# A decoder trunk on one core: where eight fixed weight tiles are used, and where a ring of six

## The chip, the core and the metric

The kernel runs on one core of one Trainium2 chip. The metric is device time in microseconds (us) of one execution; a kernel's time is the median of several runs. Profiles are of one execution each. The engines go by the profile's names: PE (matrix products), PEld (its weight loads), DVE and ACT (elementwise work), POOL, and SP, which here issues nearly all transfers from device memory.

## The reference, cut to what matters

Two pre-norm layers over a residual stream of 256 positions by 2048 columns, in 32-bit floats:

```
for layer in range(2):
    xn  = rms_norm(h, norm_mix[layer])
    mix = swa_mlstm_mixer(xn, ...) if layer == 0 else forgetting_attention_mixer(xn, ...)
    h   = h + mix                  # each mixer ends in: concat(heads) @ w_out   (2048 x 2048)
    h   = h + (silu(xn2 @ w_gate) * (xn2 @ w_up)) @ w_down     # xn2 = rms_norm(h, norm_ffn)
return rms_norm(h, norm_final)
```

Layer 0's mixer projects `xn` once and feeds a sliding-window attention (columns 0 to 1023 of the concatenation) and an mLSTM of four heads (columns 1024 to 2047). Layer 1's mixer is a causal attention of 16 heads with a forget-gate bias. An FFN has 5632 hidden columns.

## The kernel before

**A product.** Every operand is split into a rounded part `hi` and a remainder `lo`, and a product of 32-bit floats is three matmuls: `hi` with `hi`, `hi` with `lo`, `lo` with `hi` (L220 to L222 in `gemm`, L530 to L532 in `three`). Weights come in *chunks* of 256 rows by 512 columns (512 KB). SP loads a chunk into a `raw` tile (L132), ACT casts it to `hi` (L185), DVE subtracts to get `lo` (L186). A chunk then serves 12 matmuls of 512 columns: two groups of 128 rows, two halves of the 256 positions, three products. `raw` tiles for plain chunks come from the pool `wr`, four of them, and one is free again when `lo` has been computed.

**Weight slots.** A cast chunk lives in a *slot*, a pair of tiles `hi`, `lo` of 4 KB a partition each. Before the change there are six fixed pairs, made once (L104), and `slot()` (L106) hands them out in turn: a chunk's cast must wait until the matmuls on the chunk that used that pair before are done. `close_layer` (L762) opens a pool `fp`, makes two more fixed pairs in it, `more`, appends them to the six, and so has eight for everything until it ends: the output projection (`out_proj`, L508) and the FFN. Then the two are taken out again.

**Where `more` lies.** Pools are stacked. `fp` begins at the address at which the mixer's pool began (`ev` in layer 0, `od` in layer 1), as that pool has been closed by then. Within a pool, tiles lie in the order in which their tags were first asked for. `more` comes right after `sx` (two tiles of 6 KB) and `x4` (1 KB), so it takes the bytes from 13312 to 29696 of the region. In `od` those bytes hold `vtail`, the forget-gate columns, `qt`, `kt` and most of `tt`, all of them read by the last group of four heads; in `ev` they hold part of `og`, the gates, `alibi` and `dt_`, which the mLSTM reads to its end. The framework makes the first write of a tile wait for the last reader of what lay there.

**Mixers.** `project` streams a column block of 512 through `gemm`, eight chunks. `pair_group` (L537) handles two column blocks at once with eight steps, three or four of them *mixed* (a scheme that trades one of eight products for additions on DVE), the others plain. Each step of a mixer takes two slots.

**Output projection.** `out_proj` goes through the four column blocks of `w_out` two at a time. For the first two, called acc 0 and acc 1 here: the first six chunks of acc 0 (rows 0 to 1535), the first six of acc 1, then the last two of acc 0 and the last two of acc 1. In layer 1 the first six chunks of a block need none of the last group of heads; in layer 0 the first four need no mLSTM head. A block's matmuls add up in one accumulator, so that its first chunk must come first. Acc 1's first two chunks are the seventh and the eighth to ask for a slot, and with eight pairs they get `more`.

**Order.** The framework orders the instructions of each engine once, when the program is built, by a simulated timeline: an engine takes the earliest instruction in program order among those that are ready. On the chip each engine, SP's queue included, follows that order and waits where it must. The last heads of layer 1 run through scores (L384, L387), exponentials (L418), scaling (L431), transposes (L471, L475), the products with the values (L485, L486) and the split into `mh` and `ml` (L354, L355); layer 0's through L1081 to L1103, transposes on SP (L333) for two heads and on PE (L1130) for the others, and L359, L360.

Of the kernel before, what the change touches and what calls it, by code (L numbers as in the profile page):

```python
# [9 lines left out]
F32R = mybir.dt.float32r  # L10
# [7 lines left out]
P = 128  # L18
# [5 lines left out]
NB = 512  # L24
CK = 2
# [43 lines left out]
def mixed_of(order):  # L69
    return [p for w, p in order if w]  # L70
# [5 lines left out]
def trunk(  # L76
# [23 lines left out]
    xl = sp_.tile([P, KT, S], F32R, name="xl")  # L100
    mh = sp_.tile([P, KT, S], F32R, name="mh")
    ml = sp_.tile([P, KT, S], F32R, name="ml")
    wp = ctx.enter_context(tc.tile_pool(name="wp", bufs=1))
    weights = [[wp.tile([P, CK, NB], F32R, name=f"{a}{i}") for a in ("hi", "lo")] for i in range(6)]  # L104

    def slot():  # L106
        weights.append(weights.pop(0))
        return weights[-1]

    wr = ctx.enter_context(tc.tile_pool(name="wr", bufs=4))  # L110
    cp = ctx.enter_context(tc.tile_pool(name="cp", bufs=1))
# [70 lines left out]
    def split_chunk(raw, n):  # L182
        hi, lo = slot()
        for k in (slice(0, 1), slice(1, CK)) if any(raw is f for f in fine) else (slice(0, CK),):
            latest[0] = nc.scalar.copy(hi[:, k, 0:n], raw[:, k, 0:n])  # L185
            nc.vector.tensor_tensor(  # L186
                out=lo[:, k, 0:n], in0=raw[:, k, 0:n], in1=hi[:, k, 0:n].bitcast(F32), op=ALU.subtract
            )
        return hi, lo
# [318 lines left out]
    def out_proj(w, idx, key, extra):  # L508
        last, rest = KT - 4, []
        for n0 in (0, 2):  # L510
            accs = [new_acc() for _ in range(2)]
            for i in range(2):
                gemm(accs[i], m_of, w, (n0 + i) * NB, NB, 0, last, KT, step=6 * i)
            for i in range(2):
                gemm(accs[i], m_of, w, (n0 + i) * NB, NB, last, KT, KT, step=6)
                add_out(accs[i], n0 + i)
                (later if n0 == 0 else rest).append(
                    (LATER[n0 + i], split_turned(idx, n0 + i, *scrap(extra[3], n0 + i), extra))
                )
                square_sum(key, n0 + i)  # L520
        return rest
# [15 lines left out]
    def pair_group(fp, par, lhs, sums, mats, order, todo=(), halves=None, inner=None, raws=None):  # L537
# [32 lines left out]
        for pos, (kind, pair) in enumerate(order):  # L570
# [21 lines left out]
            if first:  # L592
# [8 lines left out]
                else (t4[:, 0, :], t4[:, 1, :], ra[:, 0, :], ra[:, 1, :])  # L601
            )
            hu, lu = slot()
            split_plain(hu[:, 1, :], lu[:, 1, :], rb[:, 1, :])
            nc.vector.tensor_tensor(out=ta, in0=rb[:, 0, :], in1=ra[:, 0, :], op=ALU.subtract)
# [4 lines left out]
            for src in (ra, rb) if halves else (t4, ra):  # L610
                if halves:
                    hs, ls = halves.pop(0)
                    halves.append((hs, ls))
                else:
                    hs, ls = slot()
                split_plain(hs, ls, src)
                parts.append((hs, ls))
# [144 lines left out]
    def close_layer(layer, w_out, idx, key, **rest):  # L762
        with tc.tile_pool(name=f"fp{layer}", bufs=2) as fp:
            nx = len(mixed_of(ORDER))
            nd = max(len(mixed_of(o)) for o in DOWN.values())
            sx = [fp.tile([P, nx, 4, P], F32R, name=f"sx{i}", bufs=1) for i in range(2)]
            x4 = fp.tile([P, 2, P], F32R, name="x4", bufs=1)
            more = [[fp.tile([P, CK, NB], F32R, name=f"{a}{i}", bufs=1) for a in ("hi", "lo")] for i in (6, 7)]
            weights.extend(more)
            todo = out_proj(w_out, idx, key, (*sx, x4, fp))  # L770
            sd = [fp.tile([P, nd, 4, P], F32R, tag=f"sd{i}", name=f"sd{i}", bufs=1) for i in range(2)]
            ffn(layer, fp, sx, x4, sd, key, todo, **rest)
            for pair in more:
                weights.remove(pair)


    acc0 = new_acc()
    hi, lo = slot()
# [366 lines left out]
    for n in range(4):  # L1145
        nc.gpsimd.dma_start(h[:, :, n * NB : (n + 1) * NB], xv[:, :, n * NB : (n + 1) * NB])

    close_layer(0, w_out_even[0], 2, "f0", idx_next=1, key_next="m1")


# [140 lines left out]
    def finish(acc, n, gf):  # L1291
        for t in range(NT):
# [31 lines left out]
            nc.scalar.dma_start(ov[:, t, NB : 2 * NB], b1)  # L1324

    close_layer(1, w_out_odd[0], 3, "f1", finish=finish)


# [47 lines left out]
```

## Time and profile before

| | |
|---|---|
| median of 3 runs | 2105.7 us (2105.07 to 2107.09) |
| profiled execution, own time | 2104.5 us |
| its span | 2102.8 us |
| PE busy, share of the span | 2072.5 us, 99% |
| DVE, ACT busy | 1821.5 us (87%), 1373.8 us (65%) |
| device memory read | 408.68 MB, 195 GB/s |
| mean granted PE clock | 0.993 |

How to read it: a row of the windows view gives a stretch of time in us from the span's start, then each engine's busy time in it with the number of instructions in brackets, the granted clock of PE as a share of full speed, the DMA engines' busy share and the rate. A row of the timeline gives start, duration, engine, line, operation, out<-in, shape and count, and in square brackets the engine's idle time before it with what ended it. The profiled execution's own time is 1.7 us longer than its span; the rest lies outside what the profile shows. PE counts as busy while any of its pipelined matmuls is under way.

### The profile page before, as it was taken

How to read it: one execution, taken by the hardware profiler on the slowest of the kernel's cores; microseconds unless marked ns; L12 is line 12 of the kernel's file. 1: busy time of each engine (PE TensorE's matmuls, PEld its weight loads, DVE VectorE, ACT ScalarE, POOL GpSimd, SP SyncE). 2: the span in 40 equal slices, each digit the busy share in tenths (PEclk: the TensorE clock that was granted, in tenths of full speed). 3: DMA queues.
4: the chain of work that ended last, by engine and by line, in shares of the span. 5: the costliest groups of instructions: out<-in, count | busy, mean ns of one | idle time of the engine just before them, and what ended most of it. 6: DMA issues, size and time to landing. Idle time of an engine off the chain costs nothing.

```text
span 2102.8 us, 26924 instructions
## 1 busy us (share of the span) xinstructions
PE 2072.5 (99%) x9473; PEld 1718.5 (82%) x9473; DVE 1821.5 (87%) x2367; ACT 1373.8 (65%) x1744; POOL 41.4 (2%) x66
## 2 busy tenths in 40 slices
PE   9999899999999999999999999899999999999998
PEld 7878688888888888888888888688888888888887
DVE  6788668999999899999898778579999999899994
ACT  6767577665576656667676776577655667556763
POOL 1010100000000000000000000000000000000000
PEclk9999999999999999999999999899999999999999
DMA  8566577666677567766677866476756677666763
GB/s 291 178 200 200 170 230 218 214 210 200 207 224 227 185 202 227 229 202 181 213 214 193 242 184 193 135 237 204 240 192 225 196 209 225 216 200 206 224 193 139
DMA packets 309576, 434.87 MB, mean 207 GB/s; under 512 B 106413, under 2 KB 114625, under 8 KB 309313
## 3 DMA queue, kind: packets, MB, share of 16 engines
q1 hardware_dynamic: 307088, 426.27, 66.1%
q0 software_dynamic: 1632, 5.80, 0.8%
q8 instruction: 74, 1.21, 0.2%
q10 hardware_dynamic: 720, 1.09, 0.1%
q14 instruction: 62, 0.50, 0.1%
HBM read 408.68 MB, written 2.12 MB: 195 GB/s over the span
## 4 chain that ended last, share of the span: by engine, by line
PE 94%; ACT 2%; DVE 2%; DMA 1%; issue 1%; SPq 1%; POOLq 0%; POOL 0%; ACTq 0%; DVEq 0%
PE acc L530 20%; PE acc L531 20%; PE acc L532 20%; PE acc L221 5%; PE acc L220 5%; PE acc L222 5%; PE prod L530 5%; PE prod L532 5%; PE prod L531 5%; DVE lo L186 1%; PE p L384 1%; PE po L485 1%; ACT hi L185 1%; ACT s L418 0%; DMA raw<-in_w_out_odd_dram 0%
## 5 line engine op out<-in xcount | busy, mean ns | idle before, releaser
L186 DVE TENSOR_TENSOR lo<-raw,hi 128x1024 fp32r<-128x1024 f32 (+3 forms) x656 | 769.1, 1190 | 159.2 <-ACT hi L185 157.5
L185 ACT CAST hi<-raw 128x1024 fp32r<-128x1024 f32 (+3 forms) x656 | 662.4, 1027 | 353.9 <-PE acc L532 165.3
L531 PE MATMUL acc<-lo,xh 128*128 128x512 f32 x1320 | 513.9, 389 | 0.0
L532 PE MATMUL acc<-hi,xl 128*128 128x512 f32 x1320 | 511.2, 389 | 0.0
L530 PE MATMUL acc<-hi,xh 128*128 128x512 f32 x1320 | 506.2, 390 | 0.0
L532 PEld LDWEIGHTS acc<-hi,xl 128*128 128x128 f32 x1320 | 247.8, 188 | 51.4
L531 PEld LDWEIGHTS acc<-lo,xh 128*128 128x128 f32 x1320 | 247.8, 188 | 51.4 <-issue 0.2
L530 PEld LDWEIGHTS acc<-hi,xh 128*128 128x128 f32 x1320 | 247.8, 188 | 51.4 <-issue 0.2
L354 ACT CAST hi<-raw 128x512 fp32r<-128x512 f32 x204 | 166.9, 819 | 159.5 <-PE acc L532 80.7
L355 DVE TENSOR_TENSOR lo<-raw,hi 128x512 fp32r<-128x512 f32 x204 | 190.2, 932 | 14.0 <-ACT hi L354 12.8
L531 PE MATMUL acc<-lo,mh 128*128 128x512 f32 x466 | 181.3, 389 | 0.0
L532 PE MATMUL acc<-hi,ml 128*128 128x512 f32 x466 | 180.7, 389 | 0.0
L530 PE MATMUL acc<-hi,mh 128*128 128x512 f32 x466 | 176.8, 390 | 1.3 <-ACT hi L185 1.3
L354 ACT CAST hi<-t 128x1024 fp32r<-128x1024 f32 x95 | 100.0, 1053 | 68.6 <-PE acc L532 40.7
L220 PE MATMUL acc<-hi,mh 128*128 128x512 f32 (+1 forms) x322 | 125.4, 393 | 7.8 <-ACT mh L359 7.3
L355 DVE TENSOR_TENSOR lo<-t,hi 128x1024 fp32r<-128x1024 f32 x95 | 115.7, 1218 | 16.1 <-ACT hi L354 15.8
L221 PE MATMUL acc<-lo,mh 128*128 128x512 f32 (+1 forms) x322 | 126.0, 392 | 0.1
L222 PE MATMUL acc<-hi,ml 128*128 128x512 f32 (+1 forms) x322 | 124.5, 392 | 0.0
L530 PEld LDWEIGHTS acc<-hi,mh 128*128 128x128 f32 x466 | 87.3, 188 | 20.2 <-ACT hi L185 2.2
L532 PEld LDWEIGHTS acc<-hi,ml 128*128 128x128 f32 x466 | 87.5, 188 | 18.2
L531 PEld LDWEIGHTS acc<-lo,mh 128*128 128x128 f32 x466 | 87.5, 188 | 18.2
L221 PE MATMUL acc<-lo,xh 128*128 128x512 f32 (+3 forms) x288 | 99.7, 347 | 0.2 <-DVE lo L186 0.2
(356 smaller groups left out, 3171.2 us busy)
## 6 DMA issues: line engine op xcount, KB each, us to landing
raw<-in_w_gate_dram SPq DMA_DIRECT2D x176, 512.0 KB, 4.4
raw<-in_w_up_dram SPq DMA_DIRECT2D x176, 512.0 KB, 4.7
raw<-in_w_down_dram SPq DMA_DIRECT2D x176, 512.0 KB, 4.7
raw<-in_w_in_odd_dram SPq DMA_DIRECT2D x88, 512.0 KB, 5.1
raw<-in_w_in_even_dram SPq DMA_DIRECT2D x51, 512.0 KB, 4.8
raw<-in_w_out_even_dram SPq DMA_DIRECT2D x32, 512.0 KB, 4.5
raw<-in_w_out_odd_dram SPq DMA_DIRECT2D x32, 512.0 KB, 4.4
hr<-in_w_in_even_dram SPq DMA_DIRECT2D x12, 512.0 KB, 4.5
```

Of the source, the lines that this page charges most:

```text
L185: latest[0] = nc.scalar.copy(hi[:, k, 0:n], raw[:, k, 0:n])
L186: nc.vector.tensor_tensor(out=lo[:, k, 0:n], in0=raw[:, k, 0:n], in1=hi[:, k, 0:n].bitcast(F32), op=ALU.subtract)
L220: nc.tensor.matmul(o, ah[:, ts], hi, start=(k == 0), stop=False)
L221: nc.tensor.matmul(o, ah[:, ts], lo, start=False, stop=False)
L222: nc.tensor.matmul(o, al[:, ts], hi, start=False, stop=(k == k_all - 1 and cs.stop == n))
L354: nc.scalar.copy(dst_h, src)
L355: nc.vector.tensor_tensor(out=dst_l, in0=src, in1=dst_h.bitcast(F32), op=ALU.subtract)
L384: nc.tensor.matmul(pq[j % 2][:, j // 2, :], q_of(j, b), k_of(j)[:, 0:cols], start=True, stop=True)
L485: nc.tensor.matmul(po, v_of(j, 0), tt[:, j, 0:2, :].rearrange("p c q -> p (c q)"), start=True, stop=False)
L530: nc.tensor.matmul(o, ah, hi, start=start, stop=False)
L531: nc.tensor.matmul(o, ah, lo, start=False, stop=False)
L532: nc.tensor.matmul(o, al, hi, start=False, stop=stop)
```

## The change

The six fixed pairs go. In their place `wp` is a pool of six buffers per tag, and `slot()` asks it for a new `hi` and a new `lo` whenever `stock` is empty; the pool gives whichever buffer is free, and a new tile's first write waits for the last reader of the tile that had it. `stock` is filled only around `ffn`: with two pairs in `fp`, now made after `out_proj` and after `sd`, and with six pairs taken from the ring. It is emptied when the FFN ends. So mixers and output projections run on the ring of six, and the FFNs on eight fixed pairs as before. `more` no longer lies behind `x4`, but behind everything that `out_proj` has asked of `fp`.

```diff
-    wp = ctx.enter_context(tc.tile_pool(name="wp", bufs=1))
-    weights = [[wp.tile([P, CK, NB], F32R, name=f"{a}{i}") for a in ("hi", "lo")] for i in range(6)]
+    wp = ctx.enter_context(tc.tile_pool(name="wp", bufs=6))
+    stock = []
 
     def slot():
-        weights.append(weights.pop(0))
-        return weights[-1]
+        if not stock:
+            return [wp.tile([P, CK, NB], F32R, tag=a, name=a) for a in ("hi", "lo")]
+        stock.append(stock.pop(0))
+        return stock[-1]
...
             x4 = fp.tile([P, 2, P], F32R, name="x4", bufs=1)
-            more = [[fp.tile([P, CK, NB], F32R, name=f"{a}{i}", bufs=1) for a in ("hi", "lo")] for i in (6, 7)]
-            weights.extend(more)
             todo = out_proj(w_out, idx, key, (*sx, x4, fp))
             sd = [fp.tile([P, nd, 4, P], F32R, tag=f"sd{i}", name=f"sd{i}", bufs=1) for i in range(2)]
+            more = [[fp.tile([P, CK, NB], F32R, name=f"{a}{i}", bufs=1) for a in ("hi", "lo")] for i in range(2)]
+            stock.extend(more + [slot() for _ in range(6)])
             ffn(layer, fp, sx, x4, sd, key, todo, **rest)
-            for pair in more:
-                weights.remove(pair)
+            stock.clear()
```

## The prediction

> **What bounds the kernel now.** I read the page first, then the waits of PE, then windows, then single stretches of the timeline. The page:
>
> ```profile
> span 2102.8 us, 26924 instructions
> PE 2072.5 (99%) x9473; PEld 1718.5 (82%) x9473; DVE 1821.5 (87%) x2367; ACT 1373.8 (65%) x1744; POOL 41.4 (2%) x66
> PE 94%; ACT 2%; DVE 2%; DMA 1%; issue 1%; SPq 1%; POOLq 0%; POOL 0%; ACTq 0%; DVEq 0%
> ```
>
> PE is the bound, and the change neither adds nor removes a matmul, a cast, a subtraction or a byte loaded. So it can only move the time in which PE stands, 2102.8 - 2072.5 = 30.3 us, and the time in which it runs slowly. PE's waits are nearly all in two places:
>
> ```profile
> PE pp L471 <- DVE s L431: 9.5, 1, 9.5
> PE acc L220 <- ACT mh L359: 7.3, 1, 7.3
> ```
>
> Both belong to the step from a mixer to its output projection, in layer 1 and in layer 0. The windows around them (columns: length, PE, PEld, DVE, ACT, POOL busy, clock, DMA share, rate), with the stretches before and after:
>
> ```profile
> 0.00:226.00 226.00, 223.94 (x1173) 184.69 (x1174) 178.23 (x290) 160.83 (x266) 20.41 (x43) 1.00 0.68 216
> 242.00:255.00 13.00, 4.20 (x17) 2.43 (x15) 6.73 (x26) 6.36 (x17) 1.42 (x2) 0.75 0.27 72
> 255.00:260.00 5.00, 5.00 (x17) 3.97 (x18) 3.19 (x9) 3.69 (x11) 0.69 (x1) 0.62 0.48 128
> 260.00:271.00 11.00, 10.82 (x50) 8.28 (x48) 7.83 (x13) 6.02 (x13) 0.69 (x1) 1.00 0.42 134
> 271.00:330.00 59.00, 59.00 (x262) 48.88 (x261) 38.76 (x51) 40.40 (x54) 0.00 (x0) 1.00 0.80 249
> 1050.00:1294.00 244.00, 243.97 (x1149) 204.45 (x1147) 206.72 (x273) 172.78 (x230) 13.71 (x12) 1.00 0.73 206
> 1318.00:1328.00 10.00, 0.47 (x2) 0.18 (x1) 6.18 (x15) 4.66 (x17) 0.00 (x0) 0.62 0.41 136
> 1328.00:1335.00 7.00, 7.00 (x29) 6.04 (x29) 1.99 (x7) 1.76 (x3) 0.00 (x0) 0.57 0.00 0
> ```
>
> The mixers (0 to 226 and 1050 to 1294) leave PE 2.06 and 0.03 us idle: nothing is to be won there. Lost at the two steps is, in layer 0, 13.00 - 4.20 = 8.8 us of standing, 0.2 in the row after next, and 5.00 x (1 - 0.62) = 1.9 us at the low clock; in layer 1, 10.00 - 0.47 = 9.5 us and 7.00 x (1 - 0.57) = 3.0 us. Together 10.9 + 12.5 = **23.4 us**, which is the most that the change can win there.
>
> **Why PE stands there.** I count what the output projection had done. One chunk has four L220 matmuls:
>
> ```profile
> 226.00:242.00 16.00, 6.09 (x16) 3.02 (x16) 1.00 0.73 267
> 242.00:255.00 13.00, 0.15 (x1) 0.15 (x1) 0.75 0.27 72
> 1294.00:1318.00 24.00, 9.55 (x24) 4.51 (x24) 1.00 0.62 190
> 1318.00:1328.00 10.00, 0.00 (x0) 0.00 (x0) 0.62 0.41 136
> ```
>
> These are windows of line 220 alone. In layer 1 it is 24, six chunks: all that acc 0 has without the last heads, and nothing of acc 1, whose six chunks need none of them either. In layer 0 it is 16, four chunks: acc 0's attention heads, and none of acc 1's four. So PE had work with no open operand but the weights. Were they there? The casts of layer 1:
>
> ```profile
> 1315.75 1.04 ACT L185 CAST hi<-raw 128x1024 fp32r<-128x1024 f32 x1 [1.30 <-DVE lo L186]
> 1319.47 1.04 ACT L185 CAST hi<-raw 128x1024 fp32r<-128x1024 f32 x1 [2.67 <-DVE mx L403]
> ...
> 1334.21 0.59 ACT L354 CAST mh<-po 128x512 fp32r<-128x512 f32 x1 [3.01 <-PE po L486]
> 1335.09 0.59 ACT L354 CAST mh<-po 128x512 fp32r<-128x512 f32 x1 [0.29 <-PE po L486]
> 1335.57 2.01 ACT L185 CAST hi<-raw 128x1024 fp32r<-128x1024 f32 x2
> ```
>
> and the last reader of `vtail` and `tt`, beside the two ends of the stall:
>
> ```profile
> 1317.72 0.40 PE L222 MATMUL acc<-hi,ml 128*128 128x512 f32 x1
> 1327.64 1.45 PE L471 MATMUL pp<-ident,s 128*128 128x128 f32 x4 [9.53 <-DVE s L431]
> ...
> 1334.67 0.38 PE L486 MATMUL po<-tt,vtail 128*128 128x128 f32 x2
> ```
>
> SP has loaded ahead:
>
> ```profile
> 1294.42 44.99 SPq L132 DMA_DIRECT2D raw<-in_w_out_odd_dram  x13
> ```
>
> Yet no chunk is cast between 1320.5 and 1335.57; then two are cast back to back, right after the last read of `vtail` and `tt` ends at 1335.05. Acc 1's first two chunks are the seventh and the eighth, and their slots are `more`, on the bytes of `vtail`, `qt`, `kt` and `tt`. I read the two casts as these. Acc 1 cannot begin before its first chunk, so the other four, cast or not, are of no use. Two of the four `raw` tiles are held by them besides, so that the rest of the loading goes through two. In layer 0 the pair comes after the last read of `og`:
>
> ```profile
> 263.27 0.88 DVE L1103 SCALAR_TENSOR_TENSOR hv<-hv,st,og 128x256 f32<-128x256 f32 x2 [0.48 <-POOL st L1101]
> 266.02 1.99 ACT L185 CAST hi<-raw 128x1024 fp32r<-128x1024 f32 x2
> ```
>
> **The change, part by part.**
>
> *The ring in the output projections* takes that wait away: a slot of `wp` depends on matmuls alone. PE gets acc 1's four chunks in layer 0 and six in layer 1. The row 271 to 330 has 59.00 us for 262 matmuls, 0.225 us each, so a chunk costs 12 x 0.225 = 2.7 us: 10.8 us of work in layer 0 for 10.9 us of loss, 16.2 us in layer 1 for 12.5 us. In layer 1 the cover suffices with 3.7 us to spare. In layer 0 it just does, and the mLSTM's instructions have to share ACT and DVE with more casts at that moment (1.0 and 1.2 us each, in the rows of L185 and L186 below), so I take 2 us off. Another 2 us I take off over both for an order of PE that was fixed in advance: a transpose that is queued a little early holds the chunks behind it. Below, the recovery could be nothing (what PE waits for is late by other causes too), above all 23.4. Sum: 23.4 - 2 - 2 = **19.4 us**.
>
> *Eight slots become six there.* Cost nothing, hidden by what is already cast: six chunks are 16.2 us of PE. The longest pause of casts that is not the stall itself is at the end of layer 1's projection, 1396.2 to 1405.83:
>
> ```profile
> 1394.23 2.00 ACT L185 CAST hi<-raw 128x1024 fp32r<-128x1024 f32 x2 [0.26 <-DMA raw<-in_w_up_dram]
> 1405.83 1.04 ACT L185 CAST hi<-raw 128x1024 fp32r<-128x1024 f32 x1
> ```
>
> 9.6 us, within the 16.2. Without that cover the difference, two chunks or 5.4 us a layer, would be the price.
>
> *The ring in the mixers.* The casts there already wait for slots; the groups of lines from 1050 to 1294:
>
> ```profile
> L185 ACT CAST hi<-raw 128x1024 fp32r<-128x1024 f32 (+1 forms) x78 | 76.4, 1004 | 37.0 <-PE acc L532 18.4 <-DMA raw<-in_w_in_odd_dram 15.2 <-issue 1.8
> L186 DVE TENSOR_TENSOR lo<-raw,hi 128x1024 fp32r<-128x1024 f32 (+1 forms) x78 | 89.8, 1169 | 27.7 <-ACT hi L185 27.7
> ```
>
> 18.4 us of ACT's idle time end with a matmul, which costs PE 0.03 us in all. Six pairs stay six pairs; what changes is which buffer a chunk gets, and so possibly the order. No row shows a ring. From below it could win the 2.06 + 0.03 us; from above I see no limit short of the slower case below. I take **+0.5 us**, nearer the windows' zero.
>
> *`more` behind `sd`, eight pairs in the FFNs.* Nothing: when the FFN begins, the mixer's tiles under `more` are long read, and its first two chunks get free pairs. The scraps of the output projection slide forward onto bytes that the last heads read, but they are first written after acc 0 has closed, which needs those heads. SP's queue keeps its entries; loads that waited for the two held `raw` tiles come earlier, and the transposes of L333 and L453 are queued among them as before.
>
> The sum: 19.4 - 0.5 = 18.9 us less. Against the profiled execution's span that is 2102.8 - 18.9 = 2083.9, its own time 2104.5 - 18.9 = 2085.6; the median of the runs is 1.2 us above that execution, so I predict **2087 us**.
>
> **A rule beside it.** The low clock after the stalls is the second term: 0.62 in the 5 us after 7.3 us of standing, 0.57 in the 7 us after 9.5. The Trainium skill, TensorE: Matmul & The Clock Gate, Part 1: The HAM clock gate, says that one idle window of about 3.4 us drops PE to half rate, until it has been busy for about as long. The trace agrees with the drop; by the page's window it would cost 1.7 us each, 3.4 in all, where the rows give 4.9.
>
> **The rivals.**
>
> *The heads stay the bound* (half is won). Acc 1 runs in the gap, but the order of PE puts the transposes (L471) or the first mLSTM chunk where they still wait. For it: the chain from the scores to L431 is long, and SP's transposes in layer 0 take 10.3 us in a row with nothing to shorten them:
>
> ```profile
> 245.84 10.34 SPq L333 DMA_TRANSPOSE hv<-room  x8
> ```
>
> Against it: in the other attentions the same order leaves PE 0.03 us idle over 244 us. Half of 23.4 is 11.7: 2105.7 - 11.7 + 0.5 = 2094.5 us.
>
> *Six slots are too few in the output projections.* Casts wait for PE 18.4 us in 78 there, 0.24 us each; if that fell through to PE in the 64 chunks of both projections, 15 us of the gain would go: 2087 + 15 = 2102 us. Against it: in the mixers, with six, it does not fall through. The Trainium skill, Perfetto Trace Analysis, Optimization Strategy, says that the same gap repeating on the engine that should be full can mean too few buffers; by that rule taking two away is the wrong way. The trace's two gaps do come from a buffer, but from its place.
>
> *The change doesn't do what it says*: acc 1's chunks still come late, since acc 0's fifth and sixth sit in two of six slots until the mLSTM ends. Four slots remain, so it would need the loads to be late as well. 2105.7 us.
>
> *Slower: overtaking in the mixers.* A fixed pair forces chunks into their order; the ring gives a free buffer to whichever cast is ready. In `pair_group` the mixed steps have their own `raw` tiles, loaded far ahead, and can take the buffers of an earlier plain chunk that lands late; PE then stands until a step ends. For it: 15.2 us of ACT's waits there end with a landing, so plain chunks do land late. The place: three mixed steps in each of seven groups, 21. It decides from 18.9 / 21 = 0.9 us each on; at half a chunk, 1.35 us, it is 28 us: 2087 + 28 = 2115 us.
>
> **How the numbers follow.** Chances: forecast 0.64, heads stay the bound 0.20, six too few 0.03, no effect 0.03, overtaking 0.10. A measurement of this kernel can tell about 0.2%, 4.2 us, from no change. Faster: 0.64 + 0.20 = 0.84; within: 0.03 + 0.03 = 0.06; slower: 0.10. The range goes from 2080 (all 23.4 us, the mixers' 2.1) to 2103, which takes in the half case and six too few and leaves out the last two and a little at the bottom. The forecast alone lies within 2080 to 2092.
>
> **What would show it.** Right: in the profile after, the two waits of PE above are gone or under 3 us; L220 in the stretch before the last heads' transposes counts more than 24 in layer 1, more than 16 in layer 0 before the first `mh` of L359; the clock stays at 1.00 there; no cast of L185 stands for the last read of `og` or `vtail`; PE idle in the mixers stays near 2 us. Wrong: the waits of L471 or L220 remain (heads), PE waits on ACT `hi` or DVE `lo` spread over the output projections (six too few) or over the mixers (overtaking).

## The result, and the profile after

The changed kernel takes **2078.0 us** (median of 4 runs, 2077.6 to 2079.0), the kernel before beside it 2105.4 us: a ratio of 0.987, with an interval of 0.985 to 0.989. The forecast was 2087 us and its range began at 2080 us; the time lies 9 us below the one and 2 us below the other.

The page after, the lines that answer to those shown of before:

```profile
span 2075.9 us, 26965 instructions
PE 2065.7 (100%) x9473; PEld 1715.1 (83%) x9473; DVE 1819.0 (88%) x2367; ACT 1373.7 (66%) x1744; POOL 44.6 (2%) x66
PE 97%; DVE 1%; ACT 1%; issue 1%; DMA 0%; POOLq 0%; POOL 0%; ACTq 0%; DVEq 0%
```

The same 9473 matmuls and 1744 instructions of ACT; PE stands 10.2 us instead of 30.3, which is 20.1 us less. But the span is shorter by 26.9 us, 6.8 more than that. The other 6.8 us had been booked as busy before (2072.5 against 2065.7).

The waits of PE after (all that the view names; columns: total us, times, longest):

```profile
PE cold L170 <- POOL ones L167: 1.2, 1, 1.2
PE acc L223 <- DVE lo L188: 0.2, 1, 0.2
PE acc L222 <- ACT hi L785: 0.2, 1, 0.2
```

The two waits of 9.5 and 7.3 us are gone, and nothing has come in their place (lines stand two lower than before: L222 is the former L220, L187 the cast L185, L473 the transpose L471). The windows after, of the same two steps:

```profile
226.00:242.00 16.00, 16.00 (x75) 13.39 (x74) 11.26 (x24) 7.59 (x17) 0.73 (x1) 1.00 0.68 247
242.00:255.00 13.00, 13.00 (x59) 10.79 (x58) 7.97 (x21) 9.26 (x22) 0.69 (x1) 1.00 0.29 78
255.00:260.00 5.00, 5.00 (x24) 4.13 (x23) 3.87 (x10) 3.53 (x6) 0.69 (x1) 1.00 0.69 193
260.00:271.00 11.00, 11.00 (x54) 9.01 (x53) 8.56 (x12) 7.02 (x14) 0.69 (x1) 1.00 0.72 254
1050.00:1281.00 231.00, 231.00 (x1091) 193.91 (x1091) 192.74 (x252) 164.15 (x221) 15.31 (x10) 1.00 0.71 209
1281.00:1305.00 24.00, 24.00 (x124) 20.47 (x123) 17.66 (x24) 13.69 (x15) 1.03 (x1) 1.00 0.63 203
1305.00:1323.00 18.00, 18.00 (x87) 14.99 (x87) 11.22 (x19) 11.02 (x25) 0.00 (x0) 1.00 0.53 165
```

Between 242 and 255 us there were 17 matmuls at a clock of 0.75; now 59 at 1.00. In layer 1 the whole way from 1281 to 1323 us is full. The windows of L222 alone, up to the last heads, first after, then the same of before (L220):

```profile
226.00:257.00 31.00, 13.86 (x34) 6.56 (x35) 1.00 0.50 168
1281.00:1317.00 36.00, 16.48 (x42) 8.05 (x43) 1.00 0.56 176
```

```profile
226.00:257.00 31.00, 7.51 (x18) 3.63 (x18) 0.86 0.51 172
1294.00:1327.00 33.00, 9.55 (x24) 4.51 (x24) 0.90 0.58 180
```

34 instead of 18, and 42 instead of 24 (a chunk has four of them): acc 1's chunks now run while the heads are still at work. The timeline of layer 1 after shows that the casts no longer stand for the last read of `vtail`:

```profile
1312.22 2.06 ACT L187 CAST hi<-raw 128x1024 fp32r<-128x1024 f32 x2
1315.95 1.05 ACT L187 CAST hi<-raw 128x1024 fp32r<-128x1024 f32 x1 [1.66 <-PE acc L224]
1320.02 1.05 ACT L187 CAST hi<-raw 128x1024 fp32r<-128x1024 f32 x1 [0.43 <-ACT tt L474]
...
1324.91 0.38 PE L488 MATMUL po<-tt,vtail 128*128 128x128 f32 x2
```

To see where the 26.9 us come from I cut both traces at the first and the last matmul of each output projection (those that read `mh` or `ml`; 384 in each):

| us of the span | before | after | less |
|---|---|---|---|
| to the first matmul of layer 0's projection | 227.20 | 227.23 | 0.0 |
| layer 0's projection | 107.26 | 94.95 | 12.3 |
| FFN of layer 0 and mixer of layer 1 | 959.91 | 959.19 | 0.7 |
| layer 1's projection | 111.12 | 98.01 | 13.1 |
| FFN of layer 1, to PE's last matmul | 689.27 | 688.18 | 1.1 |
| from there to the end | 8.02 | 8.30 | -0.3 |

25.4 of 26.9 us lie in the two steps that the prediction named.

### The profile page after: what moved, and what is told of

Same layout as the page of the kernel before. It is cut to its first block, busy times and chain, and to the rows that moved or that the text cites. A ratio compares the mean times of both kernels' runs of the same rounds, so it can differ in the third digit from the quotient of the medians.

```text
span 2075.9 us, 26965 instructions
## 1 busy us (share of the span) xinstructions
PE 2065.7 (100%) x9473; PEld 1715.1 (83%) x9473; DVE 1819.0 (88%) x2367; ACT 1373.7 (66%) x1744; POOL 44.6 (2%) x66
## 4 chain that ended last, share of the span: by engine, by line
PE 97%; DVE 1%; ACT 1%; issue 1%; DMA 0%; POOLq 0%; POOL 0%; ACTq 0%; DVEq 0%
PE acc L532 21%; PE acc L534 21%; PE acc L533 21%; PE acc L223 6%; PE acc L222 6%; PE acc L224 6%; PE prod L532 5%; PE prod L533 5%; PE prod L534 5%; PE p L386 1%; PE po L487 1%; ACT s L420 0%; PE po L488 0%; DVE lo L188 0%; DMA raw<-in_w_down_dram 0%
## 5 line engine op out<-in xcount | busy, mean ns | idle before, releaser
L187 ACT CAST hi<-raw 128x1024 fp32r<-128x1024 f32 (+3 forms) x656 | 661.7, 1027 | 341.2 <-PE acc L534 137.2
L222 PE MATMUL acc<-hi,mh 128*128 128x512 f32 (+1 forms) x322 | 125.8, 391 | 0.0
```

The lines of the kernel that those rows point to most:

```text
L222: nc.tensor.matmul(o, ah[:, ts], hi, start=(k == 0), stop=False)
```

## The experiments

Each run is set against runs of the kernel before on the same chip. A projection is taken from its first to its last matmul, as in the table above. The *blocked pairs* are `more` as they were before, made ahead of the projection in `fp`; in a *plain turn* the pairs are handed out again and again in one fixed order. One profile a run: in the runs that leave layer 0 as it was, its projection reads 107.8 to 108.3 us, before 107.3. In the order of the paragraphs below:

| run | time, us | less than before there | layer 0's, layer 1's projection, us |
|---|---|---|---|
| changed kernel again | 2077.2 | 27.2 | 94.9, 98.0 |
| blocked pairs out, plain turn of six | 2082.1 | 23.2 | 97.1, 98.2 |
| the same in layer 0 only | 2093.7 | 11.6 | 96.9, 111.0 |
| the same in layer 1 only | 2092.6 | 12.7 | 108.3, 98.2 |
| ring in mixers, eight in projections, blocked pairs first | 2130.2 | -24.9 | 88.6, 86.9 |
| the same, blocked pairs last | 2099.9 | 4.9 | 104.6, 110.3 |
| before, layer 1's `more` over `raw` | 2111.7 | -7.0 | 107.9, 111.3 |
| before, `raw` in a pool of its own | 2105.3 | -0.6 | 107.8, 111.2 |
| the same, `more` in a pool of its own over it | 2094.0 | 10.7 | 108.2, 98.1 |
| plain turn of six, FFN begins with `more` | 2081.4 | 23.0 | 96.9, 98.2 |
| ring in mixers only | 2079.4 | 25.1 | 97.1, 98.0 |
| ring in projections only | 2079.6 | 24.8 | 95.0, 98.2 |
| turn that skips the held two | 2083.4 | 21.4 | 94.9, 98.0 |
| the same, FFN's order mended | 2077.9 | 26.4 | 95.0, 98.0 |
| ring in mixers only, again | 2079.3 | 25.0 | 97.1, 98.0 |
| five pairs in projections | 2084.3 | 20.5 | 97.2, 98.0 |
| four pairs in projections | 2089.9 | 14.9 | 100.7, 98.9 |

**The changed kernel once more.**

> The changed kernel once more, beside the three below on one chip: 2077 to 2079 us. It is the yardstick for the 4 us by which the ring beat the fixed six.

2077.2 us, ratio 0.987 (0.986 to 0.989): the gain came again, 27.2 us after 27.4.

**The blocked pairs alone.** The six fixed pairs stay as before; only `more` is made after the projection.

```diff
-            more = [...]; weights.extend(more)
             todo = out_proj(w_out, idx, key, (*sx, x4, fp))
             sd = [...]
+            more = [...]; weights.extend(more)
```

> The six fixed pairs stay everywhere; only the two pairs of the FFN pool are made after the output projection, as in the changed kernel. My theory (all of the gain comes from taking those two pairs out of the output projection, the ring adds nothing): 2076 to 2082 us, both waits of PE (L471, 9.5 us, and L220, 7.3 us) gone. Rival (the ring's free choice of buffer is what wins): at least half of the 27 us is missing, 2090 us or more.

2082.1 us, ratio 0.989 (0.988 to 0.990). Its three longest waits of PE (line numbers as before):

```profile
PE acc L220 <- ACT hi L185: 1.2, 2, 0.7
PE cold L168 <- POOL ones L165: 1.2, 1, 1.2
PE acc L221 <- DVE lo L186: 0.8, 2, 0.6
```

Both long waits go without any ring. 23.2 us of the gain are the blocked pairs; by stages it is 10.2 us in layer 0's projection and 12.9 in layer 1's, against the 10.9 and 12.5 that the prediction had read as the loss. The other 4 us need the ring, so that "the ring adds nothing" did not hold.

**One layer at a time.** The same edit in layer 0 alone, then in layer 1 alone.

> As before the change, but in layer 0 alone the two pairs are made after the output projection. My theory: the step of layer 0 gains its 12 to 13 us, layer 1 keeps its wait on L431: 2091 to 2095 us. Rival (the two waits hang together, the second only moves): less than 8 or more than 18 us.

> As before the change, but in layer 1 alone the two pairs are made after the output projection. My theory: 13 to 14 us, 2090 to 2094 us, and the gain of this run and of the one for layer 0 add up to that of the changed kernel, 27 us, within 2 us. Rival: they do not add up, because part of the gain needs the ring.

11.6 us and 12.7 us, together 24.3 against 23.2: the two steps are separate and add up to what the blocked pairs give. They don't add up to the 27 us that I had expected of them, since the ring's part is in neither. Each run keeps the wait of the other layer, first the run with layer 0 alone, then that with layer 1 alone:

```profile
PE pp L471 <- DVE s L431: 10.5, 1, 10.5
```

```profile
PE acc L220 <- ACT mh L359: 7.4, 1, 7.4
```

**Eight pairs with the ring.** The changed kernel, with `stock` filled before the projection; first with `more` in front, then behind.

```diff
+            more = [...]
+            stock.extend(more + [slot() for _ in range(6)])      # then: [slot() ...] + more
             todo = out_proj(w_out, idx, key, (*sx, x4, fp))
             sd = [...]
-            more = [...]
-            stock.extend(more + [slot() for _ in range(6)])
```

> The ring of six in the mixers, but the stock of eight, with its two pairs right behind x4, is there for the output projections too. My theory: the two waits are back, 2103 to 2108 us, no better than before. Rival (the ring wins by itself): under 2095 us.

2130.2 us, 25 us slower than before. I had not thought of what comes first: with `more` in front it is acc 0's own first two chunks that get the blocked pairs, and PE has hardly anything to do until they come. The first matmul of the projection comes at 265.2 us instead of 227.2, in layer 1 at 1344.4 instead of 1294.4. The windows of this run:

```profile
227.00:250.00 23.00, 9.95 (x35) 6.84 (x33) 11.48 (x36) 9.06 (x25) 1.42 (x2) 0.81 0.42 142
250.00:265.00 15.00, 2.41 (x8) 1.36 (x8) 6.80 (x17) 8.14 (x20) 1.38 (x2) 0.50 0.10 22
```

> The ring in the mixers, and in the output projections a stock of eight again, but with the two blocked pairs behind the six, so that acc 0's six chunks get the six and acc 1's first two the blocked pairs, as in the kernel before. If the place of `more` in the order of use is the whole of the step's loss, the two long waits are back (PE on DVE s about 9 us, on ACT mh about 7 us) and the time is that of the kernel before less what the ring gives in the mixers, 2 to 3 us: 2102 to 2105 us. Rival: the ring in the mixers changes when tiles come free and so removes part of the waits: under 2098 us.

2099.9 us; PE's two waits are back, at 9.0 us and at 5.6 in two pieces:

```profile
PE pp L473 <- DVE s L433: 9.0, 1, 9.0
PE acc L222 <- ACT mh L361: 5.6, 2, 4.5
```

So the same eight pairs cost 25 us more than before in one place of the turn, and nearly what they did before in the other. The time is 2.1 us under the bottom of what I expected. Layer 0's projection, at 104.6 us, is 2.7 us shorter than before; I did not follow that.

**What the blocked pairs wait for.** The prediction read: the last reader of the bytes on which they lie. So I moved layer 1's `more` onto bytes that are read last before the projection begins, those of the attention's four `raw` tiles, by reserving room ahead of it in `fp`. (By the trace of this run they are read last at 1288.8 us, and not near 1293 as I wrote.)

```diff
+            if layer == 1:
+                fp.tile([P, 4, NB], F32, tag="c", name="room_c", bufs=1)
+                fp.tile([P, 2, NB], F32, tag="t4", name="room_t", bufs=1)
+                fp.tile([P, 4, P], F32, tag="tmp", name="room_s")
+                fp.tile([P, 96], F32, name="room_p", bufs=1)
             more = [...]
```

> The kernel before, with one thing moved: in layer 1 the pair tiles `more` lie, not over `vtail`, the transposed q and k and `tt`, but over the attention's two `raw` tiles, which are read last near 1293 us, before the projection begins. There are still eight pairs in layer 1's projection and `more` are still the seventh and the eighth. If the place is what costs, layer 1's step is recovered although the number is eight: PE's wait on DVE s in layer 1 is gone, layer 0's wait on ACT mh of about 7 us stays, and the time is near that of layer 1 changed alone, 2091 to 2094 us. Rival (it is the order or the number of pairs in the projection that costs): 2103 to 2107 us. If eight free pairs were better than six by a chunk or two, it would be under 2090 us.

2111.7 us: my reading fell. In the built program every engine has the same instructions in the same order as before; only the places of tiles differ. The wait is as long as ever, and the two casts come back to back as before (waits of PE, then the timeline of ACT, both of this run):

```profile
PE pp L471 <- DVE s L431: 9.7, 1, 9.7
PE acc L220 <- ACT mh L359: 7.5, 1, 7.5
```

```profile
1321.69 1.04 ACT L185 CAST hi<-raw 128x1024 fp32r<-128x1024 f32 x1 [2.31 <-DMA raw<-in_w_out_odd_dram]
...
1337.46 2.00 ACT L185 CAST hi<-raw 128x1024 fp32r<-128x1024 f32 x2
```

In the built program one can read what the first of the two casts waits for:

```
hi6 <- raw waits for   POOL  cb0 <- cb1 (last select)
                       ACT   tt <- pp   (last copy)
                       DVE   tt <- pp1  (last copy)
                       DMA   the five of POOL's queue into cb1 and scratch
                       DMA   raw <- in_w_out_odd
```

None of `cb0`, `cb1`, `scratch` lies under the moved tiles, and `tt` ends where they begin. The kernel before has the same list at its place. These are last uses of the attention's pool `od` as a whole; PE's last reads of it need no entry, since in ACT's order the cast comes behind the `mh` casts, which wait for them. A new theory: the first tile of a new pool that is written waits until *every* closed pool under that pool has had its last use, wherever in it the tile lies. To test it, `raw` gets a pool of its own below `od`, and layer 1's `more` a pool of its own on exactly those bytes; the control has only the first of the two.

```diff
-    with tc.tile_pool(name="od", bufs=1) as od:
+    with tc.tile_pool(name="odr", bufs=1) as odr, tc.tile_pool(name="od", bufs=1) as od:
+        odr_raws = [odr.tile([P, CK, NB], F32, name=f"odr{a}") for a in range(RAWS)]
...
+            mo = own.enter_context(tc.tile_pool(name="mo1", bufs=1))    # not in the control
+            more = [[mo.tile(...) ...] ...]
             fp = own.enter_context(tc.tile_pool(name=f"fp{layer}", bufs=2))
```

> The kernel before, with the attention's four `raw` tiles of layer 1 in a pool of their own, and layer 1's `more` in a pool of their own on exactly those bytes. Eight pairs in both projections, `more` seventh and eighth, as before. If a tile of a pool waits until every closed pool under that whole pool has had its last use, so that it is the pool and not the tile's own bytes that made `more` wait, the two casts of layer 1 now wait for nothing but `raw`: PE's wait on DVE s in layer 1 is gone, layer 0's on ACT mh of about 7 us stays, layer 1's projection takes 98 to 99 us instead of 111, and the time is 2091 to 2095 us (as layer 1 changed alone; up to 2098 if the new layout costs the FFN what the moved tiles cost it in the run before). Rival (the order of the casts on ACT, or the number of pairs, costs): 2104 us or more, with layer 1's projection still near 111 us.

> The control: the kernel before with the attention's `raw` tiles of layer 1 in a pool of their own, and `more` left in the FFN's pool, where it lies over both closed pools. Both long waits of PE stay and the time is that of the kernel before, 2103 to 2108 us. If it is faster by more than 4 us, what the run with two own pools shows is not the wait but the layout.

The control takes 2105.3 us, its ratio is 1.000 (0.999 to 1.001), with both waits. With the own pool it is 2094.0 us (ratio 0.995, 0.993 to 0.996), layer 1's projection falls from 111.2 to 98.1 us, and in the program `hi6` waits for `raw` alone. Waits of PE, first the control, then the own pool:

```profile
PE pp L471 <- DVE s L431: 9.6, 1, 9.6
PE acc L220 <- ACT mh L359: 6.9, 1, 6.9
```

```profile
PE acc L220 <- ACT mh L359: 7.4, 1, 7.4
PE pom L1094 <- DVE hv L1102: 1.5, 1, 1.5
```

The second run still has **eight** pairs in layer 1's projection, and `more` are still the seventh and eighth. So it is neither their number nor their turn alone but the pool in which they lie. That eight free pairs take 98.1 us and six 98.0 to 98.2 also answers the question of number for layer 1. For layer 0 no such run was made; in the built program its first cast into `more` waits for a list of the same kind.

**Where the ring's 4 us are.** First, whether it is only that the FFN begins with `more` (`weights[:0] = more` in the plain turn of six):

> Fixed six as in e1, but the two pairs of the FFN pool stand first in the list, as they do in the changed kernel, so that an FFN begins with two free pairs. If the order at the start of the FFNs is what the 4 us are: 2078 to 2079.5 us. If the ring's choice of buffer outside the FFNs is it (my theory): 2081 to 2083 us, as e1.

2081.4 us, a gain of 23.0 us where the plain turn has 23.2: no. Then the ring in one half at a time. In the first run `stock` holds six pairs while the projection runs; in the second it holds six all through the mixers and is emptied for the projection. The edit of the first:

```diff
+            stock.extend([slot() for _ in range(6)])          # ring in mixers only
             todo = out_proj(w_out, idx, key, (*sx, x4, fp))
...
-            stock.extend(more + [slot() for _ in range(6)])
+            stock[:0] = more
```

> The changed kernel with the ring in the mixers alone; the output projections use six of its tiles in fixed turn. My theory: in a fixed turn acc 0's fifth and sixth chunks, which wait for the mLSTM, hold up the two chunks that come six later, so layer 0's projection loses its 2 us (94.95 us from first to last matmul in the changed kernel, 97.07 in e1) while the rest stays: 2079.5 to 2081 us. Rival (the mixers gain it): 2077 to 2079 us.

> The changed kernel with six tiles in fixed turn in the mixers and the ring in the output projections alone. My theory: layer 0's projection keeps its 95 us; 2078 to 2080.5 us. Rival (the mixers gain it): 2081 to 2083 us.

2079.4 and 2079.6 us, the first 0.1 us under what I had expected, the second within it: each half wins some 2 us over the plain turn (25.1 and 24.8 against 23.0). By stages the projection's half is all in layer 0 (97.1 against 95.0 us). The windows of the run with the plain turn in the projections, then those of the changed kernel again:

```profile
260.00:265.00 5.00, 4.04 (x18) 2.57 (x16) 4.20 (x6) 3.74 (x7) 1.68 (x1) 1.00 0.39 127
265.00:271.00 6.00, 5.60 (x25) 4.63 (x26) 5.41 (x8) 3.21 (x5) 0.00 (x0) 1.00 0.65 212
```

```profile
260.00:265.00 5.00, 5.00 (x27) 4.03 (x25) 3.72 (x6) 2.57 (x8) 0.69 (x1) 1.00 0.83 308
265.00:271.00 6.00, 6.00 (x30) 4.99 (x29) 4.86 (x6) 4.25 (x7) 0.00 (x0) 1.00 0.67 197
```

43 matmuls against 57 in 11 us. The built program shows why. The ring's pairs, called A to F by their bytes, in the order in which the chunks of layer 0's projection get them:

```
ring:        acc 0  E A F C D B    acc 1  E A F C E A    acc 0  F C    acc 1  D B    ...
plain turn:  acc 0  1 2 3 4 5 6    acc 1  1 2 3 4 5 6    acc 0  1 2    acc 1  3 4    ...
```

Acc 0's fifth and sixth chunk (D and B) need the mLSTM's output and sit on their pairs until it comes. The ring passes over them and goes through the other four once more; the plain turn gives acc 1's fifth and sixth chunk just those two. In layer 1, where nothing is held, the ring's order is a plain turn as well, and the projection takes 98.0 us either way. To test it, the ring's order of layer 0 is written out as a fixed list (`seats`, from which `slot()` reads which of the six comes next).

```diff
+            six = [slot() for _ in range(6)]
+            stock.extend(six)
+            seats.extend([] if layer else [0, 1, 2, 3, 4, 5, 0, 1, 2, 3, 0, 1, 2, 3] + 3 * [4, 5, 0, 1, 2, 3])
             todo = out_proj(w_out, idx, key, (*sx, x4, fp))
...
+            stock[:] = more + six
```

> The ring in the mixers, and six pairs in the output projections whose turn in layer 0 is written out: acc 0's six chunks take the six, acc 1's and the following two take the first four only, twice, and after these the turn goes on with the fifth and the sixth. If what the plain turn of six costs in layer 0 is that acc 1's fifth and sixth chunk wait for the two pairs that acc 0's mLSTM chunks hold, layer 0's projection takes 95 us as with the ring, not 97, and the time is that of the changed kernel, 2077 to 2078 us. Rival (the ring wins by something else): 97 us and 2079 to 2080 us.

Layer 0's projection took 94.9 us, as foretold, but the whole 2083.4 us: 963.1 us between the projections (the ring in the mixers only: 958.7) and 1.8 us more in the last FFN than that run. The list had a second edit in it. `more + six` lets the FFN go on with the pair that was used last but three (in layer 1 last but one), where the other runs go on with the one used longest ago. With that mended:

```diff
-            stock[:] = more + six
+            stock[:] = more + (stock if layer else six[4:] + six[:4])
```

> As the run before with the turn written out, but the FFNs go on with the pair that was used longest ago (there they went on with the first of the list, one of the two or four pairs used last). If the held two pairs are the ring's whole gain in the projections: layer 0's projection 95 us, the rest as in the changed kernel, and 2077 to 2078 us, 2 us less than with the plain turn of six. If the order in which the FFN begins was not the cause of the loss in the run before, it stays at 2082 us or more.

> The ring in the mixers and a plain turn of six in the projections once more, beside the mended run on the same chip: 2079 to 2080 us, 97 us for layer 0's projection.

2077.9 us with a projection of 95.0 us, and 2079.3 with 97.1 on the same chip. The held two are the ring's gain in layer 0's projection, 2.1 us, of which 1.4 reach the whole. The pair with which the FFNs begin was worth some 5 us (gains of 21.4 and 26.4).

The mixers' half is small pieces. The run with a plain turn there (the ring in the projections only) has these waits, of which the changed kernel has only 0.2 us of the second:

```profile
PE acc L223 <- DVE c L1233: 1.5, 1, 1.5
...
PE acc L223 <- ACT hi L788: 0.4, 1, 0.4
PE p L387 <- ACT ktf L341: 0.4, 1, 0.4
```

They sum to 2.3 us, 2.1 more than there, where 2.4 us separate the two runs. The longest stands just ahead of the first matmul of layer 1's projection, at 1282.6 us. The waits name DVE and ACT; why the turn makes these late I did not test.

**Fewer pairs.** The changed kernel with only four or five pairs, in a plain turn, in the projections (`stock.extend([slot() for _ in range(4)])` before them, the rest added behind).

> The changed kernel with only four pairs, in a fixed turn, in the output projections; with six in a fixed turn there it took 2079.4 us. If six are more than is needed, four cost nothing in layer 1 (four chunks are 10.8 us of PE, a cast and a subtraction of a chunk are together some 4.5 us), and in layer 0, where two of the four are held by acc 0's fifth and sixth chunk until the mLSTM's output comes, some us: 2080 to 2086 us. Rival (six are just enough, and the count binds at once below it): PE waits on ACT hi and DVE lo in the whole of both projections, 2090 us or more.

> As the run with four pairs, with five. If six are more than is needed: 2079 to 2081 us, the same as with six within 0.1%. If the count binds just below six: more than 2082 us, between six and four.

2089.9 us, between the two expectations, and 2084.3 us, in the rival's numbers. (A cast and a subtraction are 1.0 and 1.2 us by the rows shown with the prediction, 2.2 us together and not the 4.5 that I wrote.) But the loss is not where the rival put it. Five pairs leave the projections at 97.2 and 98.0 us, where six in a plain turn have 97.1 and 98.0; four cost 3.6 us in layer 0 and 0.9 in layer 1. The rest lies behind the projections: with five, 961.6 us from layer 0's to layer 1's, against 958.7 with six. Both runs hand the FFN its pairs in another order, the unused ones last, and show PE's wait on ACT's `c` that the run with the list not mended has too (first five pairs, then that run):

```profile
PE prod L532 <- ACT c L555: 1.7, 1, 1.7
```

```profile
PE prod L535 <- ACT c L558: 2.3, 2, 1.4
```

That this order is the cause here as there I take to be likely; no run of four or five pairs with it mended was made.

## Why the prediction was right, and where it was wrong

In short: the mechanism was right, and two terms of the sum were mis-sized. The term of the output projections was 19.4 us and measured 25.4; the ring in the mixers was to lose 0.5 us and won some 2.

*The bound, and why PE stands there.* Right. Both waits belonged to chunks without a pair; with the pairs free, PE runs acc 1 under the last heads (34 and 42 matmuls of L222 where there were 18 and 24), and the clock stays at 1.00 there. As an upper end ("which is the most that the change can win there") the 23.4 us were wrong: 25.4 us came from the two steps, 1.4 more than read in layer 0 and 0.6 more in layer 1. The windows counted standing and low clock only; the last section finds 1.9 us of loss that was booked as busy, and I take the 2.0 us to be these, though no run takes them apart. That the blocked pairs alone gave 23.2 us, so near to 23.4, is luck: that run has a plain turn of six, which in layer 0 loses 2.1 us of its own. The turn of eight before did not have that loss; it gave acc 1's fifth and sixth chunk the third and the fourth pair, which nothing held.

*What the two casts wait for.* "Right after the last read of `vtail` and `tt` ends": the moment was right, the reason not. In layer 1 they wait for the whole closed pool; other bytes of the same pool changed nothing, a pool of their own took the wait away (111.2 to 98.1 us). So the sentence ahead of the prediction, that the first write of a tile waits for the last reader of what lay there, falls short for a pool opened over a closed one. The forecast did not suffer, since the change moves the tiles' first write behind the heads either way.

***The term of the output projections* ("23.4 - 2 - 2 = 19.4 us") is the first failed step.** It measured 25.4 us, 6.0 more. 4.0 of these are its two deductions ("I take 2 us off", "another 2 us I take off"), of which neither came: casts of the projection and instructions of the mLSTM share ACT and DVE between 242 and 271 us without PE standing at all (13.00, 5.00 and 11.00 us of the three rows), and no wait of PE on a transpose or its source is left. The other 2.0 are the bound above.

***The ring in the mixers, "I take +0.5 us"*, is the second.** It had a sign, and the other one. "From below it could win the 2.06 + 0.03 us" was about the size: the ring in the mixers won 2.1 us beside a plain turn in the projections (25.1 against 23.0) and 2.4 beside the ring there (27.2 against 24.8). In the second pair most of it is one wait of 1.5 us where layer 1's mixer ends.

The two together, 25.4 + 2.1 to 2.4, are 27.5 to 27.8 us, where 18.9 were forecast and 27.4 measured. The lower end of the range, 2080 us, has neither deduction in it, but 23.4 and 2.1 us; the time lies under it because 23.4 was no upper end.

*Eight slots become six.* Costed at nothing, and right for layer 1: 98.1 us with eight free pairs, 98.0 to 98.2 with six, 98.0 with five; four show it first. In layer 0 a plain turn of six pays the 2.1 us of the held pairs, which the ring does not (97.1 and 95.0 us); eight free pairs were not tried there. The Trainium skill, Perfetto Trace Analysis, Optimization Strategy, reads a gap that repeats on the engine that should be full as a possible want of buffers. Here the two gaps came not from a want of buffers but from two pairs in a pool that was not yet free; the runs show no gain from a number above five in layer 1's projection.

*`more` behind `sd`.* Costed at nothing; nothing in the waits of after belongs to it. That it comes first in the FFN's stock is worth nothing by the run made for that (23.0 against 23.2 us).

*The rivals.* The heads are not the bound (no wait of L473 or L222 on `mh` is left). Six are not too few. The change does what it says; the rival had seen that acc 0's fifth and sixth chunk sit on two pairs, and with the ring the other four are enough, as the prediction said. Overtaking in the mixers did not show: from 1050 to 1281 us PE is busy 231.00 of 231.00 us. What spoke for it, a ring that gives a free buffer to whichever cast is ready, is the very property that won 2.1 us in layer 0's projection. Whether it also won the mixers' 2 us is not shown.

## What to carry to other kernels

A tile that is laid over a pool just closed can stay blocked until the last use of that whole pool, however early its own bytes were read; give early tiles a pool of their own on early bytes, or don't use them before. A fixed turn of buffers hands a held buffer to the next chunk in line, where a ring passes over it. The place in the turn decides what a blocked pair costs: some 50 us here in the first two places and some 20 in the seventh and eighth, both against six pairs in a plain turn. The pair with which the next stage begins can count too (some 5 us). And the idle time and low clock that windows show are not the most that an edit can win there: they gave 23.4 us where 25.4 came.

## What was not expected of the hardware

PE's busy time was a poor measure of what could still be won: 99% before, and yet 1.3% came off, a quarter of it (6.8 of 26.9 us) out of busy time. 4.9 us of the 6.8 are the low clock, which the prediction had counted. The other 1.9 us I put to matmuls that stand alone and count as busy until their modelled end: the row from 260 to 271 us books 10.82 us for 50 matmuls before, and 11.00 us for 54 after, both at a clock of 1.00. No run takes this apart. The Trainium skill, Perfetto Trace Analysis, Identifying the Most-Contended Engine, says that the matmuls' busy share is a poor measure of how near a kernel is to its limit, since they are pipelined, and that the weight loads' share is better. The trace agrees with the first; the second it doesn't show, since PEld too went up by one point only, from 82% to 83%, as PE went from 99% to 100%.

In the run with `more` moved over `raw`, all matmuls of the last FFN were some 1% farther apart, with PE never idle. Its window, and the same stretch of the kernel before:

```profile
1700.00:1900.00 200.00, 200.00 (x875) 164.07 (x874) 185.41 (x218) 122.41 (x133) 0.00 (x0) 1.00 0.68 211
```

```profile
1698.00:1898.00 200.00, 200.00 (x884) 165.65 (x883) 186.78 (x222) 123.16 (x134) 0.00 (x0) 1.00 0.67 209
```

875 against 884 matmuls at the same clock of 1.00. That is 5.3 us over this FFN (650.8 us from the last matmul of the projection to the first of the last group, before 645.5) and most of that run's 7 us. Only the places of tiles in layer 1 differ, with the same order of instructions on every engine; which of them matters was not tried.
